# A hybrid decoder block on one core: a fifth SwiGLU pair by seven quarter products, and a tile pool for the recurrence's gates

## The chip, the cores and the metric

The kernel runs on one core of one Trainium2 chip. The metric is the device time of one execution, in microseconds, lower is better. Times of several runs are given by their median. One further execution was profiled; the views below read its trace.

## The reference, cut to what matters

The input is x, 512 positions of 1024 channels (float32). Two mixers run side by side, then a SwiGLU channel mixer:

```python
h = rmsnorm(x, norm1_g)
z_glu, z_rx, z_rg, z_ga, z_gb = split(h @ w_in + b_in)      # 2048, 1280, 1280, 1024, 1024 wide
u = z_glu[:, :1024] * sigmoid(z_glu[:, 1024:])
u = silu(layernorm(causal_depthwise_conv(u, 31 taps)))
y_a = u @ conv_w_out + conv_b_out
xb = causal_depthwise_conv(z_rx, 4 taps)
r, i = sigmoid(xb @ wa + ba), sigmoid(xb @ wx + bx)         # 16 heads of 80 channels
a = exp(-8 * r * softplus(-lam))
hb = scan: h[t] = a[t] * h[t-1] + sqrt(1 - a[t]**2) * i[t] * xb[t]
y_b = (hb * gelu(z_rg)) @ lru_w_out
x = x + (sigmoid(z_ga) * y_a + sigmoid(z_gb) * y_b) @ w_mix_out
h = rmsnorm(x, norm2_g)
x = x + (silu(h @ ffn_w1) * (h @ ffn_w3)) @ ffn_w2          # 2816 inner channels
return rmsnorm(x, norm_f_g)
```

## The kernel before

Channels lie on the 128 partitions, positions along the free axis, so a tile is 128 channels by 512 positions. Every float32 operand is split in a high and a low part (`split`, L115–125: ACT copies, another engine subtracts), and a product is three matmuls, high·high, high·low, low·high (`mm3`, L428).

The stages in the order of TensorE (PE):

- 0–28 us: norm1 and its transposes.
- 28–327 us: the input projection, one tile of 128 output channels (24 matmuls of 512 columns) at a time, in an order written out by hand (`ORDER`, L201). `u` is a tile of the gated convolution input (`glu`, L653), `rx` of the recurrence's input (`rx`, L667, with a 4-tap convolution on VectorE, DVE, and a copy of some rows by DMA into `ext` for heads that straddle tiles), `g` the two gate products of eight or twelve matmuls (`gates`, L702–732), `r` the recurrence (`recur`, L736–741: square root, product, scan), `rg` the product with the gelu. The 31-tap convolution (`beside`, L584) runs between them on DVE, a step at a time, for two channel tiles at once; each starts by an ACT operation (L593) and ends by an ACT copy (L599).
- 327–382 us: `yb`, the recurrence's output product; 382–426 us: `ya`, the convolution's; 426–461 us and a little after: the mixing product.
- 461–513 us: norm2, transposes, and the first SwiGLU pair.
- 513–703 us: the other ten SwiGLU pairs.
- 703–814 us: the output product, and the last norm.

**SwiGLU pairs.** The 2816 inner channels are 22 tiles. Pair k is the tiles k and k+11 of w1 and of w3. Pair 0 comes first, in halves. Pairs not in `SEVEN` are four products of 24 matmuls with 512 columns, `f` (L1057–1061), 96 in all. Pairs in `SEVEN` (`ffn_seven`, L1007–1050) treat the pair as a two by two block product and form it by seven products of quarters instead of eight, `fr`, each 24 matmuls with 256 columns, 168 in all. Four of the seven use sums of weight quarters (t1 to t4). These are made during the input projection (`make_f_sums`, L314–351): for each pair 4 steps, each with four loads of 128 KB (`fws`), four operations on GpSimd (POOL) and four stores of 128 KB (`ft`) to device memory. A step starts every third item of `ORDER`; loads and stores are issued by SyncE's queue (SP), each behind the newest load of a weight chunk (`issue_after`). A seven-pair then loads seven chunks of 512 KB, a normal one four.

**Output sums.** The output product is formed by seven products as well (`Sevenfold`, L806). `outq.make_sums(k)` (L276) prepares its weight sums for pair k: two loads of 512 KB into the `raws` buffers, four DVE operations, four stores of 256 KB. `out_sums` (L955) spreads the eleven of them over the SwiGLU stage:

```python
if k in SEVEN:
    ffn_seven(k)
    out_sums(k % 2)
    continue
...
out_sums(2 if k < KF - 1 else KF)
```

**Pools.** `longt` has 65 tiles of 128x512 float32 (L95) and holds whatever lives long: `xb`, `u`, the gates' `th{j}` and `ea{j}` (L721, L725), later `os1p`, `oe`, `ou`, `ov` of the output product (L821–833). `shortt` has 5. `raws` has 4 buffers, the split weights 5, PSUM 6 and 2 banks. A tile must wait until an older one of its pool is free. Except in the stretches marked `manual_schedule`, a scheduler orders the instructions of each engine; it knows when pool tiles come free, so a change of a pool moves instructions on every engine.

`gates(j)` works so: two banks of products; ACT makes `th` by tanh (L722), tanh of the other bank (L723), `ea` by exp (L726) and a tanh into the first bank (L727); DVE then does L728 to L731, of which L731 writes `th` again. `recur` reads both. All of L728–L731 and L740–L741 stand on DVE's queue, in order, together with the convolution's steps (L596).

Of the kernel before, what the change touches and what calls it, by code (L numbers as in the profile page):

```python
# [28 lines left out]
NF = DF // P  # L29


SLOTS, SHORT = 65, 5
RAW = 4
HL = 5
AHEAD = 4
# [5 lines left out]

SEVEN = (2, 3, 4, 5)
SUMS_AT, SUMS_STEP, SUMS_LAG, STORE_LAG = 4, 3, 2, 5


# [33 lines left out]
def tile_block(ctx, tc, a, out):  # L81
# [9 lines left out]
    def tiles(tag, bufs):  # L91
        p_ = pool(tag, bufs)
        return lambda name, dtype=F32: p_.tile([P, T], dtype, tag=tag, name=name)

    longt, shortt = tiles("long", SLOTS), tiles("short", SHORT)  # L95

    def pairt(name, dtype=F32R):

# [2 lines left out]
    def bank(name):  # L101
        return psum.tile([P, T], F32, tag="mm", name=name)
# [9 lines left out]
    def sub(eng, o, x, y):  # L112
        return eng.tensor_tensor(out=o, in0=x, in1=y, op=ALU.subtract)  # L113

    def split_to(h, l, full, eng, copy=act.copy):  # L115

        copy(h, full)  # L117
        last = sub(eng, l, full, h.bitcast(F32))
        if eng is pool_e:
            newest["sub"] = last.ins  # L120
        return h, l

    def split(name, full, eng, p_=None, copy=act.copy):
        p_ = p_ or pairt(name)
        return split_to(*p_, full, eng, copy)
# [35 lines left out]
    def weights(key, ahead=AHEAD):  # L161
        i = next(i for i, c in enumerate(chunks) if c[0] == key)
        emit_to(i + 1 + ahead)
        return held.pop(key)
# [131 lines left out]
    KF = NF // 2  # L296
    f_sums = {(n, k): dram.tile([P, 1024], F32, tag=f"f{n}_{k}", name=f"f{n}_{k}") for k in SEVEN for n in ("t1", "t2", "t3", "t4")}

# [15 lines left out]
    def make_f_sums():  # L314

        todo = [(k, i, c) for k in SEVEN for i in range(2) for c in (0, 2)]
        sums_due, stores_due = [], []
# [33 lines left out]
    for k in range(KF):  # L353
        if k in SEVEN:
            for n in ("b11", "b21", "b22", "t2", "t1", "t3", "t4"):
# [183 lines left out]
    ab, e, s, s2, po, c4 = (sm[:, i, :] for i in range(6))  # L539
# [162 lines left out]
    def gates(j):  # L702
        hv, lv = (gate_view(v[:, 0, :]) for v in weights(f"gate{j}"))
        j5 = j % 5
        banks = []
        for g in range(2):
            ps = bank(f"g{j}_{g}")
            (wh, oh), (wl, ol) = ((v[:, g, 0, :], v[:, g, 1, :]) for v in (hv, lv))
            xh, xl = xbp[j]
            mms = [(wh, xh), (wh, xl), (wl, xh)]  # L710
            if j5 % 2:
                eh, el = ext[j]
                mms += [(l[:MANY], r[:MANY]) for l, r in ((oh, eh), (oh, el), (ol, eh))]
            else:
                mms.append((oh[: 3 * FEW], ext[j][0][: 3 * FEW]))
            for k, (l, r) in enumerate(mms):
                pe.matmul(ps, l, r, start=k == 0, stop=k == len(mms) - 1)  # L717
            banks.append(ps)

        r_, i_ = banks  # L720
        th = longt(f"th{j}")  # L721
        act.activation(th, r_, AF.Tanh, scale=0.5, bias=bh[:, 0, j : j + 1])  # L722
        act.activation(i_, i_, AF.Tanh, scale=0.5, bias=bh[:, 1, j : j + 1])  # L723

        A = longt(f"ea{j}")  # L725
        act.activation(A, th, AF.Exp, scale=c8[:, j : j + 1], bias=c8[:, j : j + 1])  # L726
        act.activation(r_, th, AF.Tanh, scale=c4[:, j : j + 1], bias=c4[:, j : j + 1])  # L727
        vec.scalar_tensor_tensor(out=r_, in0=A, scalar=1.0, in1=r_, op0=ALU.add, op1=ALU.mult)  # L728
        vec.scalar_tensor_tensor(out=xb[j], in0=i_, scalar=1.0, in1=xb[j], op0=ALU.add, op1=ALU.mult)
        vec.tensor_scalar(out=A, in0=r_, scalar1=1.0, scalar2=None, op0=ALU.add)  # L730
        vec.scalar_tensor_tensor(out=th, in0=A, scalar=1.0, in1=r_, op0=ALU.add, op1=ALU.mult)  # L731
        rec[j] = A, th

    rec = {}

    def recur(j):  # L736
        A, m2 = rec.pop(j)
        mu = bank(f"mu{j}")
        act.activation(mu, m2, AF.Sqrt, scale=-0.25)
        vec.tensor_tensor(out=mu, in0=xb[j], in1=mu, op=ALU.mult)  # L740
        vec.tensor_tensor_scan(xb[j], A, mu, 0.0, op0=ALU.mult, op1=ALU.add)  # L741
# [17 lines left out]
    for kind, j in ORDER:  # L759
        next(f_sums_steps, None)  # L760
        if kind == "u":
            glu(j)
        elif kind == "rx":
            rx(j)
            run_beside(4)
        elif kind == "g":
            gates(j)
        elif kind == "r":
            recur(j)
        elif kind == "rg":  # L770
            rg(j)
            run_beside(6)
        elif kind == "gb":
            sig(GB, j, sgb, "sgb")
            run_beside(6)
        else:
            sig(GA, j, sga, "sga")
            run_beside(8)
# [27 lines left out]
    class Sevenfold:  # L806
# [14 lines left out]
        def pair(self, k, ua, va):  # L821

            n = self.name
            u_ = split(f"{n}us{k}", ua, vec)
            s1 = shortt(f"{n}s1{k}")[:, LO]
            add(s1, va[:, LO], va[:, HI])
            sp = longt(f"{n}s1p{k}", F32R)
            split_to(sp[:, LO], sp[:, HI], s1, vec)
            e = longt(f"{n}e{k}")
            sub(vec, e[:, HI], ua[:, LO], va[:, LO])  # L830
            sub(vec, va[:, LO], s1, ua[:, LO])
            sub(vec, e[:, LO], ua[:, HI], va[:, LO])
            self.ops.append((u_, sp, e, va))
# [58 lines left out]
    for n, j in enumerate(mixq.order()):  # L892
# [3 lines left out]
        o = sga[j]  # L896
# [110 lines left out]
    def ffn_seven(k):  # L1007
        u_, v_ = longt(f"ou{k}"), longt(f"ov{k}")

        def product(ps, x_, w_, again=False):  # L1010

            h, l = weights(f"f{w_}_{k}")
            for i in range(2):
                for c, (xh, xl) in enumerate(f_in[x_]):
                    for m, (lw, rx_) in enumerate(((h, xh), (h, xl), (l, xh))):
                        pe.matmul(  # L1016
                            ps[:, HALVES[i]], lw[:, 4 * i + c, :], rx_, start=not (again or i or c or m),
                            stop=bool(i and c == 3 and m == 2), skip_group_check=True,
                        )

        def out_of(c, dst):
            act.activation(c[:, LO], c[:, LO], AF.Silu)
            vec.tensor_tensor(out=dst, in0=c[:, LO], in1=c[:, HI], op=ALU.mult)

        r1, r2, r3, r5, r7 = bank(f"fr1_{k}"), bank2(f"fr2_{k}"), bank(f"fr3_{k}"), bank2(f"fr5_{k}"), bank(f"fr7_{k}")
        product(r1, "a11", "b11")
        c11 = shortt(f"c11_{k}")
        act.copy(c11, r1)
        product(r2, "a12", "b21")
        add(c11, r2, c11)  # L1030
        out_of(c11, u_[:, LO])
        product(r3, "s4", "b22")
        product(r1, "s2", "t2", True)
        q = shortt(f"q_{k}")
        act.copy(q, r1)
        product(r5, "s1", "t1")
        add(q, r5, q)
        c12 = shortt(f"c12_{k}")
        add(c12, r3, q)
        out_of(c12, u_[:, HI])  # L1040
        product(r7, "s3", "t3")
        c21 = shortt(f"c21_{k}")
        act.copy(c21, r7)
        add(q, r7, q)
        out_of(q, v_[:, HI])
        product(r1, "a22", "t4", True)
        add(c21, r1, c21)
        out_of(c21, v_[:, LO])
        o7.uv.append((u_, v_))
        o7.pair(k, u_, v_)  # L1050

    for k in range(1, KF):
        if k in SEVEN:
            ffn_seven(k)
# [104 lines left out]
```

## Time and profile before

| | |
|---|---|
| median of 3 runs | 815.35 us (814.31 to 815.55) |
| profiled execution | 816.61 us |
| its span | 814.8 us |
| mean granted clock of TensorE | 0.993 |
| PE, DVE, ACT, POOL busy | 801.8, 648.0, 445.2, 210.2 us |
| moved by DMA | 153.47 MB, mean 188 GB/s |

The span runs from the first to the last instruction of the profile; 1.8 us of the execution lie around it. Busy times are sums over one engine's instructions, so an engine at 98% is idle for 2% of the span. The granted clock is the share of TensorE's full clock that it was given.

### The profile page before, as it was taken

The numbers are of one execution on the slowest core, as the hardware profiler recorded it, in microseconds if no ns is written. First come the engines' busy times: TensorE is split into PE (matmuls) and PEld (weight loads), VectorE is DVE, ScalarE is ACT, GpSimd is POOL, SyncE is SP. The second block draws the span as 40 slices with busy tenths as digits, with TensorE's granted clock in tenths as the row PEclk, the third lists the DMA queues.
The fourth block names the chain that finished last, engine by engine and source line by source line (L and its number), as shares of the span: only waits on it lengthen the run. The fifth ranks groups of instructions, "written<-read, shape, count | busy, mean of one in ns | idle before, by whom it ended". The sixth has DMA issues, their size and how long they took to land.

```text
span 814.8 us, 11572 instructions
## 1 busy us (share of the span) xinstructions
PE 801.8 (98%) x4038; PEld 683.9 (84%) x4038; DVE 648.0 (80%) x1010; ACT 445.2 (55%) x627; POOL 210.2 (26%) x156
## 2 busy tenths in 40 slices
PE   8999999999999999999999999999999999999996
PEld 7988888887788888888888898999988888888885
DVE  4699899999999987787868869797866665688556
ACT  7546688777668855554336454374632233476443
POOL 3565778758665740000000042000000000000000
PEclk9999999999999999999999999999999999999998
DMA  7746466567565532358737525788778788576552
GB/s 209 192 123 163 131 186 204 169 192 194 163 190 156 167 88 65 101 174 256 234 106 245 156 92 177 243 251 262 227 237 264 251 286 283 185 261 210 173 167 104
DMA packets 183309, 153.47 MB, mean 188 GB/s; under 512 B 13799, under 2 KB 151443, under 8 KB 183251
## 3 DMA queue, kind: packets, MB, share of 16 engines
q1 hardware_dynamic: 183251, 152.73, 61.1%
q8 instruction: 32, 0.52, 0.3%
q14 instruction: 26, 0.21, 0.1%
HBM read 123.46 MB, written 26.21 MB: 184 GB/s over the span
## 4 chain that ended last, share of the span: by engine, by line
PE 92%; DVE 3%; DMA 1%; issue 1%; SPq 1%; POOL 0%; ACT 0%; POOLq 0%
PE z L437 31%; PE f L437 19%; PE or L840 13%; PE fr L1016 10%; PE yb L437 7%; PE ya L437 5%; PE mxr L840 5%; PE g L717 2%; DMA raw_in<-in_w_in_dram 1%; DVE cv L596 1%; SPq L393 1%; PE th L477 0%; DVE xb8l L113 0%; SPq L386 0%; POOL hl_in L113 0%
## 5 line engine op out<-in xcount | busy, mean ns | idle before, releaser
L596 DVE SCALAR_TENSOR_TENSOR cv<-u,par,cv 128x511 f32<-128x511 f32 (+17 forms) x240 | 162.8, 730 | 1.1 <-ACT cv L593 0.9
L113 POOL TENSOR_TENSOR hl_in<-raw_in,hl_in 128x1024 fp32r<-128x1024 f32 x52 | 125.4, 2415 | 92.7 <-ACT hl_in L117 90.2
L117 ACT CAST hl_in<-raw_in 128x1024 fp32r<-128x1024 f32 x52 | 54.2, 1043 | 10.2 <-PE z L437 6.6
L117 ACT CAST hl_f<-raw_f 128x1024 fp32r<-128x1024 f32 x28 | 29.3, 1051 | 51.4 <-DMA raw_f<-in_ffn_w_dram 37.7
L113 DVE TENSOR_TENSOR hl_f<-raw_f,hl_f 128x1024 fp32r<-128x1024 f32 x28 | 36.3, 1308 | 16.4 <-ACT hl_f L117 16.4
L990 POOL TENSOR_TENSOR hf<-h20h,h20l 128x512 f32<-128x512 f32 x1 | 1.3, 1287 | 172.4 <-DVE h20l L481 172.4
L117 ACT CAST hl_ob<-raw_ob 128x1024 fp32r<-128x1024 f32 (+1 forms) x23 | 23.4, 1016 | 38.9 <-PE or L840 18.6
L437 PE MATMUL z<-h10h,hl_in 128*128 128x512 f32 (+1 forms) x112 | 42.9, 385 | 1.5 <-DVE xb L741 1.2
L113 DVE TENSOR_TENSOR hl_ob<-raw_ob,hl_ob 128x1024 fp32r<-128x1024 f32 (+1 forms) x23 | 27.1, 1177 | 20.3 <-ACT hl_ob L117 20.2
L437 PE MATMUL z<-h11h,hl_in 128*128 128x512 f32 (+1 forms) x112 | 42.2, 378 | 0.0
L437 PE MATMUL z<-h12h,hl_in 128*128 128x512 f32 (+1 forms) x112 | 41.9, 376 | 0.0
L437 PE MATMUL z<-h15h,hl_in 128*128 128x512 f32 (+1 forms) x112 | 41.7, 374 | 0.0
L437 PE MATMUL z<-h14h,hl_in 128*128 128x512 f32 (+1 forms) x112 | 41.7, 374 | 0.0
L437 PE MATMUL z<-h13h,hl_in 128*128 128x512 f32 (+1 forms) x112 | 41.7, 374 | 0.0
L437 PE MATMUL z<-h16h,hl_in 128*128 128x512 f32 (+1 forms) x112 | 41.7, 374 | 0.0
L437 PE MATMUL z<-h17h,hl_in 128*128 128x512 f32 (+1 forms) x112 | 41.7, 374 | 0.0
L113 POOL TENSOR_TENSOR fws<-fws 128x256 f32<-128x256 f32 x48 | 36.3, 756 | 2.4
L113 DVE TENSOR_TENSOR ows<-ows,ows 128x512 f32<-128x512 f32 x22 | 15.2, 690 | 19.8 <-DMA ows<-in_ffn_w_dram 19.7
L113 DVE TENSOR_TENSOR hl_ot<-raw_ot,hl_ot 128x1024 fp32r<-128x1024 f32 (+1 forms) x17 | 20.1, 1191 | 11.8 <-ACT hl_ot L117 11.4
L117 ACT CAST hl_ot<-raw_ot 128x1024 fp32r<-128x1024 f32 (+1 forms) x17 | 17.5, 1028 | 17.2 <-PE or L840 15.5
L437 PEld LDWEIGHTS z<-h10h,hl_in 128*128 128x128 f32 x112 | 21.4, 191 | 6.3 <-ACT g L723 1.6
L437 PEld LDWEIGHTS z<-h11h,hl_in 128*128 128x128 f32 x112 | 21.4, 191 | 3.9
(905 smaller groups left out, 2582.3 us busy)
## 6 DMA issues: line engine op xcount, KB each, us to landing
raw_in<-in_w_in_dram SPq DMA_DIRECT2D x52, 512.0 KB
raw_f<-in_ffn_w_dram SPq DMA_DIRECT2D x28, 512.0 KB
ows<-in_ffn_w_dram SPq DMA_DIRECT2D x22, 512.0 KB
ot<-ows SPq DMA_DIRECT2D x44, 256.0 KB
raw_ob<-in_ffn_w_dram SPq DMA_DIRECT2D x33, 256.0 KB
raw_ot<-ot SPq DMA_DIRECT2D x33, 256.0 KB
fws<-in_ffn_w_dram SPq DMA_DIRECT2D x64, 128.0 KB
ft<-fws SPq DMA_DIRECT2D x64, 128.0 KB
```

The costliest lines, as they stand in the source:

```text
L113: return eng.tensor_tensor(out=o, in0=x, in1=y, op=ALU.subtract)
L117: copy(h, full)
L393: nc.sync.dma_start(xt[t][h], x_nat[:, t, h * T : (h + 1) * T])
L437: pe.matmul(ps, l, r, start=i == 0, stop=i == n - 1)
L596: vec.scalar_tensor_tensor(out=acc[c][:, s:], in0=u[c][:, : T - s], scalar=dw(c, s), in1=acc[c][:, s:], op0=ALU.mult, op1=ALU.add)
L717: pe.matmul(ps, l, r, start=k == 0, stop=k == len(mms) - 1)
L840: pe.matmul(banks[i], l_[:, ts], r_, start=start and n == 0, stop=stop and n == 2, skip_group_check=again)
L990: pool_e.tensor_tensor(out=v, in0=h2p[c][0].bitcast(F32), in1=h2p[c][1].bitcast(F32), op=ALU.add)
L1016: pe.matmul(ps[:, HALVES[i]], lw[:, 4 * i + c, :], rx_, start=not (again or i or c or m), stop=bool(i and c == 3 and m == 2), skip_group_c ...
```

## The change

The first settings change, a pool is added, and three kinds of tiles come from it:

```diff
-SLOTS, SHORT = 65, 5
+SLOTS, SHORT, GATES = 59, 5, 6
...
-SEVEN = (2, 3, 4, 5)
+SEVEN = (2, 3, 4, 5, 6)
...
-    longt, shortt = tiles("long", SLOTS), tiles("short", SHORT)
+    longt, shortt, gatet = tiles("long", SLOTS), tiles("short", SHORT), tiles("gate", GATES)
...
-        th = longt(f"th{j}")
+        th = gatet(f"th{j}")
...
-        A = longt(f"ea{j}")
+        A = gatet(f"ea{j}")
...
-            e = longt(f"{n}e{k}")
+            e = (gatet if n == "o" and k < GATES else longt)(f"{n}e{k}")
```

Pair 6 becomes a seven-pair: `ffn_seven(6)` takes the place of its four products, its seven chunks are loaded in place of four, its four steps of `make_f_sums` are added, and `out_sums(0)` follows it instead of `out_sums(2)`. Six of the long tiles become a pool of their own. The gates' `th{j}` and `ea{j}` take its tiles in turn (three gates at a time), and once the recurrence is over, the `e` tiles of the first six pairs of the output product. The computation is the same; the order of instructions that the scheduler makes is another one on ACT, DVE, POOL and SP, and on PE the same but for pair 6. Line numbers after L32 are one higher in the changed kernel.

## The prediction

> **What bounds the kernel now.** I read the page's busy times, slices and chain first:
>
> ```profile
> span 814.8 us, 11572 instructions
> ...
> PE 801.8 (98%) x4038; PEld 683.9 (84%) x4038; DVE 648.0 (80%) x1010; ACT 445.2 (55%) x627; POOL 210.2 (26%) x156
> ...
> PEclk9999999999999999999999999999999999999998
> ...
> PE 92%; DVE 3%; DMA 1%; issue 1%; SPq 1%; POOL 0%; ACT 0%; POOLq 0%
> ```
>
> TensorE (PE) is busy for 98% and makes 92% of the chain. So time falls only if PE gets less work, or loses one of its few waits. The list of PE's waits names two in the middle, and the timeline of PE shows their place:
>
> ```profile
> PE z L437 <- DVE xb L741: 1.2, 1, 1.2
> ...
> PE g L717 <- DVE th L731: 0.6, 1, 0.6
> ```
>
> ```profile
> 202.80 0.40 PE L717 MATMUL g<-ext,hl_gate 96*128 96x512 f32 x1
> 203.82 0.50 PE L717 MATMUL g<-xb7h,hl_gate 128*128 128x512 f32 x1 [0.63 <-DVE th L731]
> ...
> 206.24 0.77 PE L437 MATMUL z<-h10h,hl_in 128*128 128x512 f32 x1 [1.22 <-DVE xb L741]
> 206.80 0.63 PE L437 MATMUL z<-h10l,hl_in 128*128 128x512 f32 x1
> ...
> 209.72 0.39 PE L437 MATMUL z<-h12h,hl_in 128*128 128x512 f32 x1
> ```
>
> The eight matmuls of gate 7 take 202.01 to 206.24, 4.23 us; gate 5's eight take 159.30 to 161.15, 1.85 us. Lost: 2.4 us. From 206.24 to 209.72 eight matmuls then take 3.48 us where eight at 0.2267 take 1.81; lost: 1.7. Starts lie 0.43 apart there. The table of stretches says why: mean clock 0.79 over these 8 us, so some 3.4 us at half speed.
>
> ```profile
> 202.00:210.00 8.00, 6.16 (x19) 4.36 (x19) 8.00 (x12) 7.44 (x9) 5.20 (x6) 0.79 0.47 138
> ...
> 276.00:340.00 64.00, 64.00 (x283) 52.94 (x283) 49.20 (x68) 36.25 (x49) 14.81 (x7) 1.00 0.32 97
> ...
> 594.00:703.00 109.00, 109.00 (x482) 90.26 (x481) 63.42 (x104) 30.53 (x41) 0.00 (x0) 1.00 0.77 252
> ```
>
> (Busy us of PE, PEld, DVE, ACT, POOL; clock; DMA share; GB/s.) VectorE (DVE) is full in 202–210: its strict queue is what PE waited for. The place costs **4.1 us**. Why late: gate 6's last matmul ended near 184.9, but its tanh (L722) ran at 192.31, because its `th6` had no long slot until an older tile was freed; ACT's timeline has idle time ahead of it. L728–L731 of gate 6 so sat at 200.66–203.77 on DVE, ahead of the scan of xb4 (204.89–207.13 with its twin) for which `z25` waits.
>
> **The change, part by part.** Durations are of the profiled execution, 816.61 us (span 814.8 and 1.8 around it), 1.26 above the median 815.35; I carry differences over to the median.
>
> *Pair 6 by seven products.* The timeline has matmuls of 256 columns (L1016) start 0.120 apart and those of 512 (L437) 0.2267 apart:
>
> ```profile
> 582.28 0.28 PE L1016 MATMUL fr<-hs_0h,hl_ft 128*128 128x256 f32 x1
> 582.40 0.28 PE L1016 MATMUL fr<-hs_0l,hl_ft 128*128 128x256 f32 x1
> ```
>
> Four such pairs last 80.63 us (513.17 to 593.80), 672 matmuls, 0.1200 each. Five normal pairs last 108.83 us, 480 matmuls, 0.2267 each. Removed: 96 × 0.2267 = 21.77. Added: 168 × 0.1200 = 20.16. **−1.6 us**, 0.2% of the time. Cover: the four seven-pairs ran without a gap with DVE at 67.2 of 81 us and DMA at 0.78. The fifth loads 3.67 MB and stands beside an output sum of 2 MB as its precedents do. Were the cover gone I would see PE wait for `hl_ft`; nothing of that is in four precedents, so I take 0, with +1 as upper end.
>
> *Its preparation* (four more steps in 276–340: 16 loads and 16 stores of 128 KB, 16 POOL subtractions at 0.756 = 12.1 us). POOL is busy 14.8 of 64 us there and idle from 316 to 461; DMA share is 0.32. On SP's queue the stores stand ahead of raw loads whose subtractions are needed more than 10 us later. I take 0; if that slack were gone, a late `hl_in` would cost 1 us (four stores at the share seen), the upper end.
>
> *The gate pool.* Long slots fall by 6, 6 go to gates: 70 slots in all as before. `th6` and `ea6` now take the slots of gate 3, free since its scan ended near 161.6, so the tanh directly follows gate 6, 7 us earlier; the new order puts L728–L731 of gate 6 ahead of where PE needs them. That removes up to **−4.1 us**.
>
> But DVE's queue is reordered earlier too, and this costs. Near 100 us, the start of the convolution tiles cv2 and cv3 now stands on ACT behind the sigmoid sg3, a 1.04-us cast and the copy of u1; in the order before, cv2's start (98.90) stood ahead of them. Walking ACT: copy u0 until 100.0, sg3 100.7, cast 101.7, copy 102.3, cv2 103.0; DVE, done with cv1 at 100.0 and u3 at 101.4, stands idle some 2.2 us. It wins back 1.4 (the 1.09 it idled at 141.5 for `hl_gate5`, and small gaps). Then, near 155, the order has six more convolution steps (six times 0.63) ahead of `xb6l` and `y1l` and three more ahead of the scans:
>
> ```profile
> 156.84 0.68 DVE L113 TENSOR_TENSOR y1l<-z,y1h 128x512 fp32r<-128x512 f32 x1
> ...
> 159.27 2.32 DVE L741 TENSOR_TENSOR_SCAN xb<-ea,mu 128x512 f32<-128x512 f32 x2
> ```
>
> `y1l` ends at 157.5 before, 162.1 after by this count; the scan of xb2 at 160.5, after 163.3; `ext5` is copied by DMA from `xb6l` (ended 153.76, after near 159) and lands near 161.8. Gate 5's first product needs `ext5` at 159.98, its second `y1l` at 160.21, `z23` the scan at 161.15. So PE stalls about 1.8 for `ext5`, then 0.1 and 0.3: **+2.2 us**, between 0 (if the scheduled steps are made up) and 3.5 (if the 1.4 isn't won back). Behind it on PE stands everything, so it counts in full.
>
> How fast the clock is behind that stall is open. Before, the half-clock stretch began at 206.21 after 2.4 us of idle within the 3.4 before it, no single gap over 1.22. Counting back from 206.21 by 3.41, stretches start at 158.43 and 161.84: 1.9 of the new idle would lie in the first. That is less than 2.4, so I take no clock loss, with 1.7 at the upper end. The Trainium skill ("TensorE: Matmul & The Clock Gate", section "Why this matters for your kernels") advises no idle gap over about 3 us, as one idle window brings half clock; by it, the new stall would cost 2.2 and no more. The trace doesn't agree with that limit, since gaps of 1.22 and less came before the half clock at 206.21.
>
> *The output sums.* L1056 makes 0 or 1 sums after a seven-pair, 2 after a normal one, the rest at the end. Pair 6 makes 0 instead of 2, so one (k=10) is left for after pair 10: 1 MB of loads, 1 MB of stores, and 4 DVE operations of 0.69 us. Its loads take the raw tiles freed at 694.3 (where SP issues an output weight before) and land some 5.2 us later, as the output weights issued at 684.15 do (cast at 689.58): 699.5. Its operations (until 702.3) stand on DVE's queue ahead of `oe9`, which ran at 698.07. From `oe9` to the next output weight's subtraction (701.4) DVE needed 3.35, then 0.75 for `ou10` and `ov10`: 706.4 instead of 703.65. The bank that `ov10` frees is needed at 706.03: **+0.4 us**, between 0 (loads two us sooner) and 2.5 (two later); the output weights behind `ov10` have 2 us and more.
>
> Sum: −1.6 − 4.1 + 2.2 + 0.4 = **−3.1 us**: 813.5 for the profiled execution, **812.3** for the median.
>
> **Rivals.**
> - *Clean removal*: the walk to 160 is too dark and the sum at 700 is hidden: −1.6 − 4.1 = −5.7, 809.6. For it: PE has covered such shifts for 300 us with one exception. Against: six steps of 0.63 ahead of `xb6l` exceed the slack of `y1l` (2.7).
> - *Half clock at 160*: as forecast, with 1.7 more: −1.4, 813.9, within 0.2%. For it: the row at 206.21, and no 3-us gap was needed there. By the page's rule it wouldn't come.
> - *The gate pool doesn't do what it says*: gate 6's steps still come late on DVE, and the stall of 204 stays, without one at 160: −1.6 + 0.4 = −1.2, 814.2. Against: the order puts them early.
> - *Slower*: DVE's queue is so late from 100 on that the stall at 160 comes with half clock (2.2 + 1.7) and DVE, still full at 202–210, keeps PE waiting at 204 as well: −1.6 + 3.9 + 0.4 = +2.7, 818.1. It decides from a net front loss of 2.8 (1.6 for the products, less 0.4, plus the 1.6 that a measurement can tell). For it: DVE busy 16.15 of 17 us in 185–202. Against: PE shifted by 2.2 needs the scan 2.2 later.
>
> **Chances.** 0.2% is 1.6 us, about what a measurement here can tell from no change. Forecast 0.40, clean 0.20 (both faster); half clock 0.15 and no effect of the pool 0.10 (both same); slower 0.15. The range: 809.5 takes in the clean case; 817.4 the upper ends of stall (1.3 more), clock (1.7) and sums (2.1) added to 812.3 (the ends of +1 for pair 6 and its preparation only in place of one of these); beyond it lies part of the slower case alone. The likeliest case's own range is 810.1 (no stall at 160) to 813.6 (its upper end).
>
> **What would show it.** Right: the seven-pairs' first row x160 instead of x128, and the normal pairs' rows x40 instead of x48; no wait of PE for th near 204; a wait near 160 for `ext5` or `y1l`; PE wait near 705 for a bank freed by `ov10`. Wrong: PE waiting for `hl_ft` in pair 6 (cover gone), the stall at 204 still there, PE clock below 1.00 in 158–166, or a wait elsewhere between 100 and 300 that the order doesn't show.

## The result, and the profile after

The changed kernel takes **818.86 us** (median of 6, 818.22 to 819.64), the kernel before 814.70 (median of 6, 813.92 to 815.55): ratio **1.0051**, 95% interval 1.0038 to 1.0064. That is 4.2 us slower; 3.1 us faster was forecast, and the time lies outside the range. The profiled execution took 819.64 us.

The page of the changed kernel, the lines that answer to those of before:

```profile
span 817.8 us, 11826 instructions
...
PE 800.2 (98%) x4110; PEld 685.3 (84%) x4110; DVE 654.9 (80%) x1018; ACT 448.4 (55%) x633; POOL 225.3 (28%) x172
...
PE 68%; DVE 12%; DMA 10%; SPq 3%; ACT 3%; issue 2%; POOL 2%; DVEq 0%; POOLq 0%; ACTq 0%
```

TensorE has 1.6 us less to do and yet ends 3 us later: it waited. Its share of the chain falls from 92% to 68%: the chain now leaves PE at its waits and runs back through other engines and DMA. The list of its waits names three that the kernel before did not have (us in total, times, longest):

```profile
PE g L718 <- DMA ext<-xb6h: 4.3, 1, 4.3
PE or L841 <- DVE ov L967: 1.3, 1, 1.3
...
PE fr L1017 <- ACT c L1029: 0.9, 1, 0.9
```

The first is at gate 5 (159 us), the second at the start of the output stage, the third inside pair 3. The two waits near 204 us are gone. The table of stretches shows both places, gate 5 and gate 7, and the preparation of pair 6 (same columns as before):

```profile
159.00:168.00 9.00, 4.69 (x14) 3.46 (x13) 9.00 (x14) 5.87 (x8) 8.62 (x7) 0.81 0.21 44
205.00:213.00 8.00, 8.00 (x37) 6.60 (x36) 8.00 (x13) 5.42 (x8) 6.46 (x6) 1.00 0.59 175
276.00:340.00 64.00, 64.00 (x284) 52.95 (x283) 52.25 (x71) 35.82 (x49) 31.22 (x23) 1.00 0.52 158
```

PE is busy for 4.69 of 9 us at gate 5, at a clock of 0.81, and for all of 8 at gate 7. In 276–340 POOL works 16 us more and PE loses nothing.

The starts of matmuls, read from the two timelines stage by stage, give the balance:

| stretch of TensorE | before | after | |
|---|---|---|---|
| until gate 5 | 159.30 | 159.03 | −0.27 |
| gate 5, eight matmuls | 1.85 | 7.42 | +5.57 |
| to gate 6 | 21.78 | 22.27 | +0.49 |
| gate 7, eight matmuls | 4.23 | 1.85 | −2.38 |
| to gate 8 | 28.91 | 27.22 | −1.69 |
| gate 6 to gate 7, and gate 8 to pair 2 | 297.09 | 297.09 | 0 |
| pairs 2 to 10 | 189.46 | 188.99 | −0.47 |
| output stage (to its last matmul's start) | 104.73 | 106.53 | +1.80 |
| sum | | | +3.05 |

(Pairs 0 and 1 both run ahead of 513 us, so the stretch from 513 to 703 holds the nine pairs 2 to 10.) The 4.2 us of the medians are 1.1 more: the profiled execution of before lay 1.9 us above its median, that of after 0.8 above its own. "Until gate 5" differs between profiles of one front by up to 2 us (157.69 to 159.69 in experiments 2 and 6), and all of that lies ahead of 28 us: from the start of the run of 240 matmuls there to gate 5 all four profiles of that front take 131.54.

**How gate 5 came to wait.** The timeline of GpSimd, then SyncE's queue, then PE (start, duration):

```profile
156.16 0.74 POOL L114 TENSOR_TENSOR fws<-fws 128x256 f32<-128x256 f32 x1
156.84 0.52 POOL L184 MEMSET raw_gate<- 128x512 f32 x1
```

```profile
157.39 2.31 SPq L189 DMA_DIRECT2D raw_gate<-in_lru_wa_dram  x5
159.74 1.04 SPq L189 DMA_DIRECT2D raw_gate<-in_lru_wx_dram  x2
160.89 0.54 SPq L698 DMA_DIRECT2D ext<-xb6h  x1
161.53 0.54 SPq L698 DMA_DIRECT2D ext<-xb6l  x1
162.11 1.22 SPq L698 DMA_DIRECT2D ext<-xb6h  x2
```

```profile
164.18 0.76 PE L718 MATMUL g<-ext,hl_gate 96*128 96x512 f32 x1 [4.31 <-DMA ext<-xb6h]
164.74 0.63 PE L718 MATMUL g<-xb5h,hl_gate 128*128 128x512 f32 x1
165.17 0.63 PE L718 MATMUL g<-xb5l,hl_gate 128*128 128x512 f32 x1
```

Read it upwards. Gate 5 needs three copies into `ext5`. `xb6l`, the last of their sources, was ready at 157.85, but SP issued the copies from 160.89 on, behind seven small loads of gate 6's weights at some 0.48 each. Those waited for a memset of their buffer on POOL, which the new order puts behind the four sums `fws` instead of ahead of three of them. In the kernel before the memset, the same loads and the copies stood here:

```profile
147.97 0.54 POOL L183 MEMSET raw_gate<- 128x512 f32 x1
```

```profile
149.46 2.38 SPq L188 DMA_DIRECT2D raw_gate<-in_lru_wa_dram  x5
151.89 2.55 SPq L188 DMA_DIRECT2D raw_gate<-in_lru_wx_dram  x5
154.55 0.54 SPq L697 DMA_DIRECT2D ext<-xb6h  x1
```

The memset is 8.9 us later. The three sums are 2.3 of that; most of the rest is older, for POOL stood idle 6.8 us until 144.19, waiting for ACT. After the wait for `ext5` the matmuls start 0.43 apart: half clock.

### The profile page after: what moved, and what is told of

Same layout as the page of the kernel before. It is cut to its first block, busy times and chain, and to the rows that moved or that the text cites. A ratio compares the mean times of both kernels' runs of the same rounds, so it can differ in the third digit from the quotient of the medians.

```text
span 817.8 us, 11826 instructions
## 1 busy us (share of the span) xinstructions
PE 800.2 (98%) x4110; PEld 685.3 (84%) x4110; DVE 654.9 (80%) x1018; ACT 448.4 (55%) x633; POOL 225.3 (28%) x172
## 4 chain that ended last, share of the span: by engine, by line
PE 68%; DVE 12%; DMA 10%; SPq 3%; ACT 3%; issue 2%; POOL 2%; DVEq 0%; POOLq 0%; ACTq 0%
PE z L438 24%; PE or L841 12%; PE fr L1017 9%; PE yb L438 7%; PE ya L438 5%; PE mxr L841 5%; PE f L438 4%; DVE cv L597 3%; DMA ows<-in_ffn_w_dram 3%; DMA raw_in<-in_w_in_dram 2%; DMA ot<-ows 2%; PE g L718 1%; DVE hl_f L114 1%; POOL hl_in L114 1%; DVE ows L114 1%
## 5 line engine op out<-in xcount | busy, mean ns | idle before, releaser
L597 DVE SCALAR_TENSOR_TENSOR cv<-u,par,cv 128x511 f32<-128x511 f32 (+16 forms) x240 | 162.4, 730 | 2.4 <-ACT cv L594 2.2
L114 POOL TENSOR_TENSOR fws<-fws 128x256 f32<-128x256 f32 x60 | 47.8, 799 | 5.0 <-DMA fws<-in_ffn_w_dram 2.3
L118 ACT CAST hl_f<-raw_f 128x1024 fp32r<-128x1024 f32 x24 | 25.1, 1051 | 36.3 <-DMA raw_f<-in_ffn_w_dram 14.9
L114 DVE TENSOR_TENSOR hl_f<-raw_f,hl_f 128x1024 fp32r<-128x1024 f32 x24 | 32.9, 1380 | 9.5 <-ACT hl_f L118 9.4
L1017 PE MATMUL fr<-hs_0h,hl_ft 128*128 128x256 f32 x160 | 29.7, 284 | 0.9 <-ACT c L1029 0.9
L114 DVE TENSOR_TENSOR hl_ft<-raw_ft,hl_ft 128x1024 fp32r<-128x1024 f32 x20 | 24.4, 1219 | 5.3 <-ACT hl_ft L118 5.3
```

Source lines behind the costliest of these rows:

```text
L597: vec.scalar_tensor_tensor(out=acc[c][:, s:], in0=u[c][:, : T - s], scalar=dw(c, s), in1=acc[c][:, s:], op0=ALU.mult, op1=ALU.add)
L1017: pe.matmul(ps[:, HALVES[i]], lw[:, 4 * i + c, :], rx_, start=not (again or i or c or m), stop=bool(i and c == 3 and m == 2), skip_group_c ...
```

## The experiments

Each is compared with the kernel before on the same chip; stage times are the starts of matmuls.

**1. The gate pool alone.**

```diff
-SEVEN = (2, 3, 4, 5, 6)
+SEVEN = (2, 3, 4, 5)
```

> The gate pool and the 59 long slots alone; four seven-pairs as before. The order of every engine up to pair 6 is that of the changed kernel. Theory Q (the loss is made in the front by the new order): the wait of TensorE at gate 5 near 159 us stands (gate 5's eight matmuls take about 7.4 us instead of 1.85, then about 0.5 us of half clock), the wait at gate 7 near 204 us is gone (-4.1 us); the SwiGLU and output stages as before. Sum about +2.0 us: ratio about 1.0025, time about 816.7 beside 814.7. Rival theory F (the fifth seven-pair, its 4 MB of preparation and its load make the loss): no loss at gate 5 and a ratio of 0.995 to 1.000.

Measured: 818.43, ratio 1.0051 (1.0039 to 1.0063). Gate 5 takes 6.77, the half clock behind it adds 1.26, gate 7 takes 1.85, pairs 2 to 10 189.46, the output stage 104.75. The whole loss is made by the new order in the front. The profile's balance from gate 5 on is +2.1, as expected; the medians differ by 4.2, since the profile of before is one of its longest executions (experiment 8), 2.4 us above its median here.

**2. The fifth seven-pair alone.** 65 long slots, `th`, `ea` and `e` from them as before.

> The fifth seven-pair alone; 65 long slots, no gate pool. The order of every engine up to pair 6's preparation is that of the kernel before. Theory Q: the front is as before, with the wait near 204 us; pair 6 gives -1.6 us, the last output sum behind pair 10 costs about 1.8 us at the start of the output stage; sum about +0.2 us, ratio 1.000 (0.999 to 1.002). Rival theory F: the loss is here, ratio 1.004 or more, with waits of TensorE in or around pair 6.

Measured: 814.75, ratio 1.0000 (0.9989 to 1.0011). Pairs 2 to 10 take 187.86, **−1.60** as worked out, and the output stage 106.06, +1.33. Theory F falls, theory Q stands.

**3. Gate loads off SyncE's queue.**

```diff
-    nc.sync.dma_start(v[r : r + nr, gi, ei, c : c + ncol], ...)
+    nc.gpsimd.dma_start(v[r : r + nr, gi, ei, c : c + ncol], ...)
```

> The changed kernel, but the small loads of the gates' weights are issued by GpSimd's queue instead of SyncE's. The orders of TensorE, VectorE and ScalarE are the changed kernel's, instruction for instruction. Theory S (gate 5 waited for the copies into ext5, which stood on SyncE's queue behind gate 6's loads and these behind a memset on GpSimd): the copies are issued as soon as xb6l ends (157.8), land near 161.0, and gate 5 waits 1.3 us, with y1l and the scan of xb2 some 1.9 us in all instead of 5.6 us and 0.5 us of half clock: time about 4 us below the changed kernel, 814.7 to 815.2, ratio about 1.000. Theory D (VectorE's order alone makes the wait): it stays at 5 us or more, ratio 1.005. Issues on GpSimd take it time of its own; if they are long, weights (hl_in) come late and TensorE waits for them.

Measured: 816.47, ratio 1.0031 (1.0019 to 1.0043). Gate 5 takes 3.77, so it waits **1.92** where 1.9 was expected. SP's queue, and PE:

```profile
156.66 0.53 SPq L698 DMA_DIRECT2D ext<-xb6h  x1
158.41 0.53 SPq L698 DMA_DIRECT2D ext<-xb6l  x1
158.99 1.22 SPq L698 DMA_DIRECT2D ext<-xb6h  x2
```

```profile
161.38 0.47 PE L718 MATMUL g<-ext,hl_gate 96*128 96x512 f32 x1 [1.03 <-DMA ext<-xb6h]
162.16 0.49 PE L718 MATMUL g<-xb5h,hl_gate 128*128 128x512 f32 x1 [0.31 <-DVE y1l L114]
```

The copies now follow `xb6l` (ended 158.39) at once, and PE waits for `ext5`, then for `y1l`, the two that the prediction named. So of the 5.6 us at gate 5, 1.9 are VectorE's order and 3.7 SyncE's queue with the half clock. The loss against before shrank from 4.2 to 2.3 us, by 1.9 and not by 4: the moved issues cost POOL 0.5 each, and PE now waits 0.7 at gate 6 and 0.7 near 207.

**4. The output sum earlier.**

```diff
-            out_sums(k % 2)
+            out_sums(1 if k in (3, 5, 6) else 0)
```

> The changed kernel with one output sum after pair 6 (after pairs 3, 5 and 6), so that none is left behind pair 10. The front is the changed kernel's. Theory O (the sum behind pair 10 delays ov10 on VectorE's queue and TensorE with it): the wait near 708 us for ov is gone, the output stage takes 105.1 us instead of 106.9: about 817.1, ratio 1.0028. Rival: the sum after pair 6 crowds the DMA queues beside the seven chunks of pair 6 and its neighbours, TensorE waits there, and the time stays at 818.9.

Measured: 817.18, ratio 1.0039 (1.0027 to 1.0051). The output stage takes 104.73, the wait for `ov` is gone, and pairs 2 to 10 take 187.86: the sum beside pair 6 costs nothing. Theory O holds.

**5. A gate pool for gates 6 to 9 only**, with the sum early.

```diff
-SLOTS, SHORT, GATES = 59, 5, 6
+SLOTS, SHORT, GATES = 61, 5, 4
...
-        th = gatet(f"th{j}")
+        th = (gatet if j >= 6 else longt)(f"th{j}")
...
-        A = gatet(f"ea{j}")
+        A = (gatet if j >= 6 else longt)(f"ea{j}")
```

> Five seven-pairs, the output sum after pair 6 as in the run before, 61 long slots, and a gate pool of 4 that only gates 6 to 9 use. The order of every engine up to gate 5 is that of the kernel before, and gate 6's steps on VectorE come early as in the changed kernel. So no wait at gate 5. Theory W (the work of VectorE ahead of the scan of xb4 is the same in any order, and VectorE is full there, so an early gate 6 only moves TensorE's wait to the scan): gate 7 runs in 1.85 us, but z25 behind it waits 1.4 to 2.2 us for the scan; time about 812 (-1.6 for pair 6, 0 to -1 in the front), ratio 0.997 to 0.998. Rival theory L (gate 6's late tanh was the whole cause): no wait near 204, -1.6 - 2.4 or more, 810 or less, ratio 0.995 or less.

Measured: **811.59**, ratio **0.9959** (0.9946 to 0.9972). Gate 5 takes 1.84 and gate 7 1.85, with full clock behind both. Theory W expected a wait of z25 and there is none: the scan of xb4 ended at 203.66, 2.4 us sooner than before. So theory W's sum of VectorE's work was wrong by some 2 us; experiments 9 and 10 show by what. Theory L has no wait near 204, as measured, but the time is above its 810; experiments 9 and 10 speak against its cause.

**6. The fifth seven-pair with the sum early, no gate pool.**

> The fifth seven-pair without the gate pool, and the output sum after pair 6. The front is that of the kernel before, with its wait near 204. If the products' gain is -1.6 and the sum behind pair 10 was all that took it back: pairs 2 to 10 in 187.9 us, the output stage in 104.7, ratio 0.998, about 812.6. If crowded DMA queues take it back: TensorE waits inside the seven-pairs, ratio 0.999 to 1.000.

Measured: 813.59, ratio 0.9983 (0.9971 to 0.9996). Pairs 187.86, output stage 104.73, gate 7 4.23 as before: the products' gain in full.

**7. Late gate pool, four convolution steps moved behind gate 7.**

```diff
-            run_beside(4)
+            run_beside({8: 2, 9: 6}.get(j, 4))
...
-            run_beside(6)
+            run_beside({3: 4, 4: 8}.get(j, 6))
```

(the first in `rx`, the second in `rg`)

> As the run with the late gate pool, and four convolution steps of VectorE (0.64 us each, 2.5 us) moved from before gate 7 (after rx8 and rg3) to behind it (after rx9 and rg4). Theory W: the scan of xb4 now ends about 2.5 us sooner, and the wait of z25 is gone: ratio 0.995, about 810.2, 1.4 to 2.2 us below the late pool alone. Theory L: no more than the late pool alone gives. If VectorE is full behind gate 7 too, the wait comes back near 238 us.

Measured: 811.00, ratio 0.9956 (0.9942 to 0.9970), not apart from experiment 5. Theory W's further gain of 1.4 to 2.2 is not there: no wait was left to remove.

**8. The kernel before once more.**

> The kernel before once more (a blank line added), for a second profile. The profiled execution took 816.61 us with a mean clock of 0.993, while over half of the executions of this kernel have 0.998 at 813.4 to 814.5. If the half clock behind the wait near 204 is a matter of where its window falls in an execution, a profile at 0.998 shows the wait of 2.4 us there and matmuls 0.227 us apart behind it; if it always follows the wait, they lie 0.43 apart for 1.7 us of loss in this one too.

Measured: 815.08, clock 0.995, with the half clock behind gate 7 (28.92 to gate 8). It was not a profile at 0.998. But experiment 6 has the same wait of 2.38 and 27.30 behind it, full clock. So the same wait brings half clock in some executions only.

The trace's record of the granted clock tells them apart. Within each profile, the stretches at half clock begin whole multiples of 3.413 us apart (8.24 and 206.21 in the first profile of before, 58 times), and the two waits fall on that grid differently. In the first profile of before, the stretch ahead of the half clock and the one at half clock (columns as in the table of stretches):

```profile
202.80:206.21 3.41, 1.59 (x6) 0.67 (x5) 3.41 (x6) 3.37 (x6) 3.25 (x4) 1.00 0.40 111
206.21:209.62 3.41, 3.38 (x8) 2.73 (x9) 3.41 (x5) 3.27 (x4) 0.84 (x2) 0.50 0.42 117
```

In experiment 6, the two stretches that hold its waits:

```profile
201.27:204.68 3.41, 2.78 (x12) 1.85 (x11) 3.41 (x6) 3.38 (x5) 3.17 (x5) 1.00 0.77 239
204.68:208.10 3.42, 2.20 (x11) 1.49 (x10) 3.42 (x5) 3.37 (x5) 2.71 (x2) 1.00 0.41 116
```

Before has both waits in one stretch, PE busy for 1.59 of 3.41 us (1.55 and 1.60 in experiments 8 and 2), and half clock follows. Experiment 6 has them in two stretches, 2.78 and 2.20, and none follows. At gate 5 the changed kernel and experiment 4 have a stretch with PE busy for 0, experiment 1 one with 0.85, and half clock follows; it does not follow those of 2.2 to 2.4 in experiments 3, 9 and 10, nor one of 1.62 in experiment 1. Where the limit lies is not shown, and no run moved the grid on purpose.

Over the 37 executions of before beside experiments 1 to 8, eleven have a mean clock of 0.998 and took 813.7 to 814.5; eight have 0.993 or less and took 815.9 to 816.7. The profile that I predicted from, 816.61 at 0.993, is one of the latter kind. (My "over half" for the former was too many, and the clock alone doesn't order them: 813.28, the shortest, has 0.996, and 816.84, the longest, 0.995.) The 1.5 us between that profile and this one are not made at gate 7, where both have the half clock. They lie ahead of 28 us: the run of 240 matmuls starts at 27.76 there and at 26.21 here, and from 8.24 to 11.65 the clock is 0.50 there and 1.00 here.

**9. and 10. GpSimd's sums moved by a little**, on experiment 6's kernel.

```diff
-SUMS_AT, SUMS_STEP, SUMS_LAG, STORE_LAG = 4, 3, 2, 5
+SUMS_AT, SUMS_STEP, SUMS_LAG, STORE_LAG = 4, 3, 1, 5
```

(experiment 10: SUMS_LAG 3)

> The run with the fifth seven-pair and the early output sum, with the sums of weight quarters on GpSimd one item of the order earlier (SUMS_LAG 1 instead of 2). The orders of TensorE, VectorE and ScalarE are unchanged, instruction for instruction; on GpSimd one operation of 0.74 us less stands between gate 7's weights and hl_in25. Theory P (xb8l on VectorE, 2.8 us instead of 0.7, is held until GpSimd's hl_in25 ends, and that makes most of the wait near 204): hl_in25 starts and ends about 0.7 us sooner, xb8l ends 0.55 behind it as in the other runs, and gate 7's eight matmuls take about 3.5 us instead of 4.23. Theory R (gate 6's late tanh alone makes the wait): 4.2 us as before. Time -0.7 by the first, within the noise.

> The same with SUMS_LAG 3: hl_in25 stands directly behind gate 7's weights on GpSimd, four operations of 0.74 us sooner, and the four follow it. VectorE's order differs in nine places, by one to three instructions each. Theory P: hl_in25 is over when xb8l starts, and xb8l takes 0.7 us, or up to 0.7 more if it meets one of the four short operations; the wait near 204 shrinks by 1.4 to 2.1 us, though gate 6's tanh is as late as before. Theory R: the wait stays at 2.4 us.

Measured: SUMS_LAG 1 812.66, ratio 0.9975 (0.9962 to 0.9988), gate 7 **3.51** instead of 4.23; SUMS_LAG 3 811.86 in its one execution, gate 7 **1.84**. VectorE's `xb8l` and GpSimd's `hl_in25` in the kernel before, then with SUMS_LAG 1, then with 3:

```profile
190.91 2.76 DVE L113 TENSOR_TENSOR xb8l<-xb,xb8h 128x512 fp32r<-128x512 f32 x1
```

```profile
190.72 2.40 POOL L113 TENSOR_TENSOR hl_in<-raw_in,hl_in 128x1024 fp32r<-128x1024 f32 x1
```

```profile
190.85 1.96 DVE L114 TENSOR_TENSOR xb8l<-xb,xb8h 128x512 fp32r<-128x512 f32 x1
```

```profile
189.86 2.40 POOL L114 TENSOR_TENSOR hl_in<-raw_in,hl_in 128x1024 fp32r<-128x1024 f32 x1
```

```profile
190.56 0.76 DVE L114 TENSOR_TENSOR xb8l<-xb,xb8h 128x512 fp32r<-128x512 f32 x1
```

```profile
188.37 2.41 POOL L114 TENSOR_TENSOR hl_in<-raw_in,hl_in 128x1024 fp32r<-128x1024 f32 x1 [1.20 <-ACT hl_in L118]
```

`xb8l` ends at 193.67 and 192.81, each time 0.55 after `hl_in25` (193.12 and 192.26); where that ended at 190.78, `xb8l` takes 0.76. Theory P holds in both. Experiment 9 is the clean one: the orders of PE, DVE and ACT are experiment 6's, `xb8l` is 0.82 shorter than there, and gate 7 is 0.72 shorter. In experiment 10 gate 6's tanh came even later than in experiment 6, here first experiment 6 and then 10:

```profile
192.67 0.68 ACT L723 ACTIVATE th<-g,bh 128x512 f32<-128x512 f32 x1
```

```profile
193.53 0.69 ACT L723 ACTIVATE th<-g,bh 128x512 f32<-128x512 f32 x1
```

And PE does not wait at gate 7. Experiment 10 has help besides: a convolution step less stands ahead of the scan, and PE comes later, because `z23` waits 1.3 at 161.7 for the scan of xb2. But `xb8l` alone gives 2.0 of the 2.4. So most of the wait near 204 was this block of 2.1 us, not the late tanh. No run has gate 6's steps early with `xb8l` still held. By experiment 5's rows the scan, which ended at 203.66 there, would then end near 205.7, and `z25`, due at 204.0, would wait some 1.7 us: an estimate, and about what theory W expected.

The Trainium skill says as much ("SBUF — State Buffer", section "Who interferes with whom"): a VectorE instruction with two SBUF inputs contends with a GpSimd instruction that reads SBUF, and the pair of ports that the two share is an exclusive lock. The trace agrees, with 0.55 us from the end of the one to the end of the other. The convolution's steps, whose second input lies in PSUM, kept 0.7 us beside the same POOL work.

## Why the prediction was wrong, point by point

- *Pair 6, −1.6*: right. 187.86 against 189.46 in experiments 2, 4, 6, 7, 9 and 10. In the changed kernel's own profile only −0.47 came through: PE lost 1.13 in pair 3, where it waits for a copy (L1029) that stands on ACT's queue behind a cast of output sums, which itself waits 1.05 for DVE. The `raw_fb` loads were issued late there, at 527.12, behind two more stores of output sums on SP; but experiment 5 issues them at 520.50 and still loses 0.61, experiment 3 loses 0.73, and the others lose nothing. So the late loads are not shown to be the cause, and what decides it from one execution to the next stays open.
- *Its preparation, 0*: right; from gate 8 to pair 2 the times agree to 0.01 us.
- *The gate pool, −4.1*: the wait went, by a cause that I had wrong. "Its `th6` had no long slot" was a true reading of ACT, but the tanh set little of the time (by the estimate under experiment 10); the busy record of `xb8l`, 2.76 us where an unhindered one of its like takes 0.68, set most of it. (Gate 6's last matmul started at 185.46, so "ended near 184.9" was a misreading by 0.9 us.) I read "DVE is full" from busy shares and didn't compare the duration with others of the same form. The new order happened to move `xb8l` off POOL's `hl_in25` (0.68 in the changed kernel).
- And its size: 1.7 of the 4.1 was half clock, which came in three of the four profiles with this wait. The step that failed is "I carry differences over to the median", which takes it for every execution. Experiment 1 speaks against that: by the stage times from gate 5 on it should lose 2.1 us if before's executions have this half clock and 3.7 if they have not, and the medians differ by 4.2 (3.2 to 5.1). The 1.3 us by which the profile lay above its median is another matter, made ahead of 28 us as far as experiment 8 shows.
- *VectorE's order, +2.2 at 160*: the mechanism and size are right for the part that was walked (1.92 in experiment 3; `y1l` ended at 161.6 in the changed kernel where 162.1 was counted, `xb6l` at 157.85 where "near 159" was). **The step that failed** is "`ext5` is copied by DMA from `xb6l` … and lands near 161.8": the walk let the copies start when their source was ready and left out the queue that issues them. SP's seven loads behind POOL's memset add some 3 us: `ext5` came at 164.1, in experiment 3 at 161.3 though the front ran 0.5 later there. The prediction walks SP's queue for the preparation at 276–340 and not here, though the new order moved gate loads and sums there too.
- *No half clock at 160*: wrong; about 1.6 us of the 6.1 is half clock. The longer wait (4.7 us from start to start) brings it where 1.9 was expected, and 1.9 brought none in experiment 3. The comparison itself was off: of the "2.4 us of idle" ahead of 206.21, the row of that stretch has 1.82 (3.41 less 1.59 busy).
- *The output sum, +0.4*: the mechanism is right, the size 1.80 in the changed kernel and 1.33 in experiment 2. The loads landed later: in the changed kernel the first of the four operations ran 1.4 us later than walked, once PE's later start is taken off.

```profile
702.17 0.69 DVE L114 TENSOR_TENSOR ows<-ows,ows 128x512 f32<-128x512 f32 x1 [3.94 <-DMA ows<-in_ffn_w_dram]
```

Put together, the forecast of −3.1 had −1.6 − 4.1 + 2.2 + 0.4. With the wait near 204 at 2.4, without half clock, the runs give −1.6 − 2.4 + 6.1 + 1.8 = +3.9, of 4.2 measured (interval 3.1 to 5.2). Of the 7.3 us between forecast and result, 3.9 are gate 5, 1.7 the half clock behind gate 7 and 1.4 the output sum. How many of before's executions have that half clock is not shown; were it all of them, the sum would be +2.2, outside the interval.

The rival "Slower" had the right sign, and its half clock at 160 came, but by the wrong path: it wanted the wait near 204 to stand as well. The trace of before could have told of the true one: the copies stood on SP's queue right behind gate 6's ten loads, issued 0.1 us after the last of them.

## What to carry to other kernels

When a change lets a scheduler reorder, walk every queue on the path of a moved operand, the queue that issues its copies first: here the path was POOL's memset, SP's seven loads, three copies, PE. Compare a busy record with others of the same form before calling an engine full, since a blocked instruction looks busy. Once neither part disturbed the front, both paid: experiment 5 is 0.41% (0.28 to 0.54) faster than the kernel before, though its gain at gate 7 comes with `xb8l` unblocked (0.68 us there) and is not the pool's alone.

## What the runs showed of the hardware

- A VectorE subtraction with both inputs in SBUF took 2.76, 1.96 or 0.76 us, by where GpSimd's 2.4-us subtraction stood; the profile counts the blocked time as busy. In the kernel before `xb7l` and `xb9l` show it too (2.22 and 2.47, each ending 0.55 or 0.56 after a GpSimd subtraction). It goes the other way as well: beside `xb5l`, which took its 0.70, GpSimd's subtraction took 3.02 instead of 2.40.
- Half clock followed the two waits near 204 (1.0 and 1.6 us from start to start) in three profiles (the kernel before twice, experiment 2) and not in experiment 6; it did not follow a single one of 1.6 or 1.4 in experiments 9 and 10, and it followed the one of 4.7 at gate 5 in the changed kernel and experiments 1 and 4. In these profiles, between 30 and 800 us, it went with PE's busy time in a whole stretch of the 3.413-us grid at full clock, and not with the longest gap: after 1.60 of 3.41 us or less half clock followed, after 2.1 or more it did not, nor after the one of 1.62. Experiment 4 then stayed at half clock for a second stretch, though PE had been busy for 2.76 in the first.
